# Row normalisation on one DMA queue: the order of loads and stores changed from alternating to runs of two

## The chip, the core and the metric

The kernel runs on one core of one Trainium2 chip. The metric is device time in microseconds (us) of one execution; lower is better. The core's engines that matter here are DVE (VectorE), ACT (ScalarE), SP (SyncE, which only issues transfers and waits) and the core's 16 DMA engines, which move the data between HBM and the on-chip memory SBUF.

## The reference: what is computed

```python
def reference(x):                      # x: 32 x 512 x 1024, float32
    sums = np.sum(np.abs(x), axis=-1, keepdims=True)
    return (x / (sums + 1e-8)).astype(np.float32)
```

Each of the 16384 rows of 1024 numbers is divided by the sum of its absolute values. x is 67.11 MB, and so is the output: every byte is read from HBM once and written once.

## The kernel before

**Tiling.** The 16384 rows are cut into 8 tiles (`ntiles`). One tile is 128 partitions x 16 rows (`R = 16`) x 1024 numbers: 8.39 MB, 64 KB in each partition, and contiguous in HBM. The tiles live in a pool of three buffers (`BUFS = 3`, line 29; pool, line 34), so tile 3 takes the buffer of tile 0, tile 4 that of tile 1, and so on: a tile's load may start only when the tile three before it has been stored. The result is written over the input in the same buffer.

**One tile's work.** `load(i)` (lines 70 to 78) issues the load on SP's queue (line 74) and then puts the tile's arithmetic, `normalize`, into the programs of DVE and ACT. DVE reduces all 16 rows to their sums of absolute values (line 40), adds 1e-8 (line 47), takes the reciprocal (line 49) and multiplies the first 8 rows by it (line 50). ACT multiplies the other 8 rows, one instruction a row (line 57), beside DVE's multiplication. `store(i)` (lines 80 to 84) issues the tile's store, also on SP's queue (line 82). The last tile, number 7, is cut into two halves of 8 rows by `span` (lines 64 to 66): two loads, two pieces of arithmetic, two stores. So there are 9 loads and 9 stores in all.

**What sets the order.** All transfers go through one queue, that of SP. SP takes its instructions in order: before a load it waits until the buffer's earlier store has landed, before a store until the tile's arithmetic is done, and whatever stands behind a waiting instruction waits too. Issued transfers go to the 16 DMA engines. The order is written out by hand as a list, `plan` (lines 88 to 95), and followed under `tc.manual_schedule()` (lines 97 to 102). With L for a load and S for a store, the list before is

```
L0 L1 L2  S0 S1  L3  S2  L4  S3  L5  S4  L6 L7  S5 S6 S7
```

Three loads come first; then a store and a load take turns; lines 94 and 95 swap the last load with the store ahead of it, so L7 stands directly behind L6. In this list a load is followed by a store at five places: L2 S0, L3 S2, L4 S3, L5 S4 and L7 S5. A store is followed by a load at four: S1 L3, S2 L4, S3 L5 and S4 L6. The arithmetic on DVE and ACT is in the order of the tiles, 0 to 7.

Of the kernel before, what the change touches and what calls it, by code (L numbers as in the profile page):

```python
# [1 line left out]

# [4 lines left out]

FP32 = mybir.dt.float32
EPS = 1e-8


@with_exitstack
def kernel(
    ctx: ExitStack,
    tc: tile.TileContext,
    x: bass.AP,
    out: bass.AP,
):
    nc = tc.nc
    P = nc.NUM_PARTITIONS  # L20

    x_flat = x.flatten_outer_dims()
    out_flat = out.flatten_outer_dims()
    n, d = x_flat.shape

    R = 16
    assert n % (P * R) == 0
    ntiles = n // (P * R)
    BUFS = 3

    x_t = x_flat.rearrange("(n p r) d -> n p r d", p=P, r=R)
    out_t = out_flat.rearrange("(n p r) d -> n p r d", p=P, r=R)

    sbuf = ctx.enter_context(tc.tile_pool(name="sbuf", bufs=BUFS))
    stats = ctx.enter_context(tc.tile_pool(name="stats", bufs=4))

    def normalize(x_tile, r0, k, kv):

        s = stats.tile([P, R], FP32)
        nc.vector.tensor_reduce(  # L40
            out=s[:, :k],
            in_=x_tile[:, r0 : r0 + k, :],
            axis=mybir.AxisListType.X,
            op=mybir.AluOpType.add,
            apply_absolute_value=True,
        )
        nc.vector.tensor_scalar_add(out=s[:, :k], in0=s[:, :k], scalar1=EPS)  # L47
        inv = stats.tile([P, R], FP32)
        nc.vector.reciprocal(out=inv[:, :k], in_=s[:, :k])  # L49
        nc.vector.tensor_mul(  # L50
            out=x_tile[:, r0 : r0 + kv, :],
            in0=x_tile[:, r0 : r0 + kv, :],
            in1=inv[:, :kv].unsqueeze(2).to_broadcast([P, kv, d]),
        )
        for r in range(kv, k):
            row = x_tile[:, r0 + r, :]
            nc.scalar.activation(  # L57
                out=row,
                in_=row,
                func=mybir.ActivationFunctionType.Copy,  # L60
                scale=inv[:, r : r + 1],
            )

    def span(i):
        k = R // 2 if i == ntiles - 1 else R
        return [(r0, k) for r0 in range(0, R, k)]

    tiles = {}

    def load(i):  # L70
        x_tile = sbuf.tile([P, R, d], FP32)
        tiles[i] = x_tile
        for r0, k in span(i):
            nc.sync.dma_start(
                out=x_tile[:, r0 : r0 + k, :], in_=x_t[i][:, r0 : r0 + k, :]
            )
        for r0, k in span(i):
            normalize(x_tile, r0, k, k // 2)

    def store(i):  # L80
        for r0, k in span(i):
            nc.sync.dma_start(  # L82
                out=out_t[i][:, r0 : r0 + k, :], in_=tiles[i][:, r0 : r0 + k, :]
            )

    plan = [("L", i) for i in range(BUFS)]
    for i in range(ntiles):
        plan.append(("S", i))  # L90
        nxt = i + BUFS - 1
        if BUFS <= nxt < ntiles:
            plan.append(("L", nxt))
    last = max(k for k, p in enumerate(plan) if p[0] == "L")
    plan[last - 1], plan[last] = plan[last], plan[last - 1]

    with tc.manual_schedule():
        for what, i in plan:
            if what == "L":
                load(i)  # L100
            else:
                store(i)


# [1 line left out]
_INS = ['x']  # L106
_OUTS = [((32, 512, 1024), 'float32')]


# [23 lines left out]
```

## Time and profile before

| | us |
|---|---|
| median of 4 runs (lowest to highest) | 318.94 (318.53 to 319.83) |
| the profiled execution's own time | 318.72 |
| its span, first to last instruction | 316.9 |
| time of the profiled execution outside the span | 1.8 |
| DVE busy (36 instructions) | 211.0, 67% of the span |
| ACT busy (65 instructions) | 68.8, 22% |
| DVE idle, waiting for a load to land (5 times) | 79.6 |
| one reduction of a whole tile, line 40 | 17.22 |
| one multiplication of 8 rows by DVE, line 50 | 8.69 |
| bytes moved (read plus written) | 134.2 MB |

The profile is one execution, taken by the hardware profiler. Its page gives each engine's busy time, a strip of 40 equal slices of the span with the busy share of the DMA engines and the GB/s they moved, the DMA queues, the chain of work that ended last, and the costliest groups of instructions. L40 is line 40 of the kernel. The trace behind the page can be asked for more: when each transfer was issued and how many us later it landed, what each engine waited for, and the busy times and GB/s in any stretch of the span that one chooses. "DMA share" in such a stretch is the mean busy share of the 16 engines; a packet is counted where it starts, so a share can come out a little above 1.

### The profile page before, as it was taken

Reading aid. Unit: us, or ns where it says so; the run is one execution under the profiler, and the core shown is the slowest. Engines: PE = TensorE matmul, PEld = TensorE weight load, DVE = VectorE, ACT = ScalarE, POOL = GpSimd, SP = SyncE. Lnnn points to the kernel's source line nnn. Section 1 sums busy time; section 2 is a strip of 40 time slices with the busy share of each in tenths; the row PEclk is TensorE's granted clock in tenths of the full one; section 3 lists DMA queues with packets and bytes.
Section 4 is the critical chain, followed back from the end, with each engine's and each line's share of the span. In section 5 each row is a group of like instructions: output and inputs, shape, how many; then the busy total and the mean of one; then the engine's idle time right before and its main releaser. Section 6 shows DMA issues by size and latency. Waiting matters only on the chain.

```text
span 316.9 us, 193 instructions
## 1 busy us (share of the span) xinstructions
DVE 211.0 (67%) x36; ACT 68.8 (22%) x65; POOL 0.2 (0%) x4
## 2 busy tenths in 40 slices
DVE  0019999999998007995089950899509999998000
ACT  0010081054028000055000550005400063415000
POOL 0000000000000000000000000000000000000000
DMA  9999999999999999999999999999999999999895
GB/s 397 397 397 488 438 397 405 389 447 480 397 397 505 422 397 414 505 405 397 414 455 455 397 455 414 447 405 455 430 397 443 426 473 414 447 422 447 380 451 244
DMA packets 2593, 134.23 MB, mean 424 GB/s; under 512 B 288, under 2 KB 288, under 8 KB 288
## 3 DMA queue, kind: packets, MB, share of 16 engines
q1 hardware_dynamic: 2592, 134.22, 98.7%
q14 instruction: 1, 0.01, 0.0%
HBM read 67.11 MB, written 67.11 MB: 423 GB/s over the span
## 4 chain that ended last, share of the span: by engine, by line
DVE 50%; DMA 29%; another core or an unknown queue 12%; issue 0%; DVEq 0%; SPq 0%
DVE s L40 33%; DMA x_tile<-in_x_dram 19%; DVE x_tile L50 17%; DMA out_dram<-x_tile 10%; DVE inv L49 1%; DVE s L47 0%; DVEq L50 0%; SPq L82 0%
## 5 line engine op out<-in xcount | busy, mean ns | idle before, releaser
L40 DVE TENSOR_REDUCE s<-x_tile 128x16 f32<-128x16384 f32 (+1 forms) x9 | 137.9, 15320 | 79.6 <-DMA x_tile<-in_x_dram 79.6
L57 ACT ACTIVATE x_tile<-x_tile,inv 128x1024 f32<-128x1024 f32 x64 | 67.5, 1136 | 200.1 <-DVE inv L49 190.7
L50 DVE TENSOR_TENSOR x_tile<-x_tile,inv 128x8192 f32<-128x8192 f32 (+1 forms) x9 | 69.7, 7744 | 0.6
L57 ACT ACT_TABLE_LOAD x1 | 1.3, 1283 | 22.7 <-DMA x_tile<-in_x_dram 22.7
L49 DVE RECIPROCAL inv<-s 128x16 f32<-128x16 f32 (+1 forms) x9 | 2.2, 242 | 0.3
L47 DVE TENSOR_SCALAR s<-s 128x16 f32<-128x16 f32 (+1 forms) x9 | 1.6, 174 | 0.3
L117 POOL MEMSET const-bfloat16-1.0<- 128x1 bf16 x1 | 0.1, 101 | 0.0
L117 POOL MEMSET const-uint8-127<- 128x1 uint8 x1 | 0.1, 101 | 0.0
L117 POOL MEMSET const-float32-0.0<- 128x1 f32 x1 | 0.1, 98 | 0.2 <-issue 0.2
L117 POOL MEMSET const-float32-1.0<- 128x1 f32 x1 | 0.1, 98 | 0.0
## 6 DMA issues: line engine op xcount, KB each, us to landing
x_tile<-in_x_dram SPq DMA_DIRECT2D x2, 4096.0 KB, 33.8
out_dram<-x_tile SPq DMA_DIRECT2D x2, 4096.0 KB, 26.1
x_tile<-in_x_dram SPq DMA_DIRECT2D x7, 51.3
out_dram<-x_tile SPq DMA_DIRECT2D x7, 32.3
```

Of the source, the lines that this page charges most:

```text
L40: nc.vector.tensor_reduce(out=s[:, :k], in_=x_tile[:, r0 : r0 + k, :], axis=mybir.AxisListType.X, op=mybir.AluOpType.add, apply_absolute_v ...
L47: nc.vector.tensor_scalar_add(out=s[:, :k], in0=s[:, :k], scalar1=EPS)
L49: nc.vector.reciprocal(out=inv[:, :k], in_=s[:, :k])
L50: nc.vector.tensor_mul(out=x_tile[:, r0 : r0 + kv, :], in0=x_tile[:, r0 : r0 + kv, :], in1=inv[:, :kv].unsqueeze(2).to_broadcast([P, kv, d]),)
L57: nc.scalar.activation(out=row, in_=row, func=mybir.ActivationFunctionType.Copy, scale=inv[:, r : r + 1],)
L117: nc = _bacc.Bacc("TRN2", target_bir_lowering=False, num_devices=1)
```

## The change

Only the list is built differently. After the three first loads, two stores and then two loads are appended, until nothing is left; the swap at the end is gone.

```diff
     plan = [("L", i) for i in range(BUFS)]
-    for i in range(ntiles):
-        plan.append(("S", i))
-        nxt = i + BUFS - 1
-        if BUFS <= nxt < ntiles:
-            plan.append(("L", nxt))
-    last = max(k for k, p in enumerate(plan) if p[0] == "L")
-    plan[last - 1], plan[last] = plan[last], plan[last - 1]
+    stored, loaded = 0, BUFS
+    while stored < ntiles:
+        for i in range(stored, min(stored + 2, ntiles)):
+            plan.append(("S", i))
+        stored = min(stored + 2, ntiles)
+        for i in range(loaded, min(loaded + 2, ntiles)):
+            plan.append(("L", i))
+        loaded = min(loaded + 2, ntiles)
```

The two lists, one under the other:

```
before  L0 L1 L2  S0 S1  L3  S2  L4  S3  L5  S4  L6 L7  S5 S6 S7
after   L0 L1 L2  S0 S1  L3 L4  S2 S3  L5 L6  S4 S5  L7  S6 S7
```

A load is now followed by a store at four places (L2 S0, L4 S2, L6 S4, L7 S6), and a store by a load at three (S1 L3, S3 L5, S5 L7). The transfers themselves, their sizes, the buffers and the arithmetic are the same. Between the landing of the last load and the end of the list there were three stores, S5, S6 and S7; now there are two.

## The prediction

> **What bounds the kernel now.** I read the page's strip of slices first, then the queue line, then the chain, then a table by stages.
>
> ```profile
> DVE  0019999999998007995089950899509999998000
> ...
> DMA  9999999999999999999999999999999999999895
> ...
> DMA packets 2593, 134.23 MB, mean 424 GB/s; under 512 B 288, under 2 KB 288, under 8 KB 288
> ...
> q1 hardware_dynamic: 2592, 134.22, 98.7%
> ```
>
> The reader is to see that the DMA row is nine tenths or more from the first slice nearly to the last, while DVE has holes. The queue's packets fill 98.7% of 16 engines' span: 0.987 x 316.9 = 312.8 us. The 4.1 us left lie before the first packet and after the last. So the DMA engines set the time, and DVE's 67% does not.
>
> The chain of waits gives landings (start plus duration): the first load 0.72 + 21.93 = 22.65, S0 49.20 + 32.56 = 81.76, L3 81.78 + 38.94 = 120.72.
>
> ```profile
> 0.72 21.93 DMA x_tile<-in_x_dram
> ...
> 49.20 32.56 DMA out_dram<-x_tile
> ...
> 81.78 38.94 DMA x_tile<-in_x_dram
> ```
>
> S0 waits 32.56 us and L3 38.94, though each is 8.39 MB: they stand in the queue behind others. The other landings I took from the view of x_tile's instructions over short windows, which gives one issue's time and its us to landing (L1: 1.1 + 40.9 = 42.0; L2: 1.6 + 60.8 = 62.4; S7's second half: 291.9 + 24.1 = 316.0). Cutting the span at these landings gives one stage for each transfer:
>
> ```profile
> 22.65:42.00 19.35, 19.22 (x4) 2.86 (x3) 0.00 (x0) 1.00 1.00 434
> 42.00:62.40 20.40, 20.40 (x2) 6.85 (x7) 0.00 (x0) 1.00 1.00 411
> 62.40:81.76 19.36, 19.26 (x5) 8.43 (x8) 0.00 (x0) 1.00 1.00 433
> 81.76:101.10 19.34, 19.24 (x4) 7.97 (x8) 0.00 (x0) 1.00 1.00 434
> 101.10:120.72 19.62, 0.72 (x1) 0.46 (x1) 0.00 (x0) 1.00 1.00 428
> 120.72:140.10 19.38, 19.19 (x4) 1.55 (x2) 0.00 (x0) 1.00 1.00 433
> 140.10:160.00 19.90, 7.15 (x1) 6.87 (x7) 0.00 (x0) 1.00 0.99 422
> 160.00:179.30 19.30, 19.11 (x4) 1.48 (x2) 0.00 (x0) 1.00 1.00 435
> 179.30:199.50 20.20, 7.22 (x1) 6.95 (x7) 0.00 (x0) 1.00 0.98 415
> 199.50:218.90 19.40, 19.20 (x4) 1.56 (x2) 0.00 (x0) 1.00 1.01 436
> 218.90:238.20 19.30, 7.14 (x1) 6.87 (x7) 0.00 (x0) 1.00 0.98 423
> 238.20:257.90 19.70, 19.49 (x4) 1.85 (x2) 0.00 (x0) 1.00 1.05 451
> ```
>
> The columns are the stretch, its length, busy DVE, ACT and POOL, clock, DMA share and GB/s. From the top: L1, L2, S0, S1, L3, S2, L4, S3, L5, S4, L6, L7. S5, S6 and S7 follow by 277.3, 296.7 and 316.0. The reader is to see two things. A transfer takes about 19.35 us (8.39 MB at 434 GB/s) whichever way it goes. And the longer ones are all loads with a store behind them: L2 is over by 1.05, L3 by 0.27, L4 by 0.55, L5 by 0.85, L7 by 0.35. A load behind a load (L1, L6), a store behind a load (S0), a store behind a store (S1) and a load behind a store (L6) cost no more than 19.36. So a turn from loading to storing has a price, 3.07 us over five, and the turn back has none I can see.
>
> **The change part by part.** *Bytes and instructions.* 9 loads and 9 stores, 36 DVE and 65 ACT instructions stay. A DMA issue on SP takes 0.33 to 0.43 us and their number is unchanged. Sum: 0.
>
> *Turns.* Five become four. L2 S0 stays as it is, 1.05: nothing ahead of it is moved. The three others (L4 S2, L6 S4, L7 S6) follow a pair of loads, or a lone load behind a pair of stores, and have no exact row. From below a turn costs 0.27, from above 1.05, by the rows. I take the mean of the four later turns, (0.27 + 0.55 + 0.85 + 0.35) / 4 = 0.505, since these stand in the same part of the run; L7's row, after the pair L6 L7, is the only one of that shape and is below it. New sum 1.05 + 3 x 0.505 = 2.57 against 3.07: **0.5 us less**. Bounds: 1.05 + 3 x 0.27 = 1.86, 1.2 less; 4 x 1.05 = 4.2, 1.1 more.
>
> *Does the queue ever run dry?* Laying the new list out with 19.35 a transfer and 0.5 a turn, from L2's landing at 62.4: S0 81.8, S1 101.1, L3 120.5, L4 140.3, S2 159.7, S3 179.0, L5 198.4, L6 218.2, S4 237.6, S5 256.9, L7 266.6 and 276.8 (halves), S6 296.1, S7 305.8 and 315.5. A transfer costs the end nothing if it is issued before the one ahead of it lands. A whole tile's arithmetic takes 17.22 + 0.2 + 0.3 + 8.69 = 26.5 us, a half 8.68 + 0.4 + 4.43 = 13.5; ACT's share lies beside DVE's multiplication.
> - L4 moves ahead of S2 on SP, and so S2 now stands behind L4's wait for S1 (101.1). S2's tile is ready at 101.8 (DVE's multiplication, 93.13 + 8.69), so the wait delays it by nothing. Both are in the queue by 102.7; L4 is needed at 120.5, S2 at 140.3.
> - S3: arithmetic 120.5 to 147.0, needed at 159.7. Cover 12.7.
> - L5 waits for S2 (159.7), needed at 179.0; L6 waits for S3 (179.0), needed at 198.4. Cover 19.
> - S4 stands behind L6's wait: ready at 173.5 (DVE takes it after tile 3), issued at 179.8, needed at 218.2. Held 6 us, and nothing waits for it.
> - S5: arithmetic 198.4 to 224.9, needed at 237.6. Cover 12.7. L7, two issues, waits for S4 (237.6), needed at 256.9.
> - S6 stands behind L7's wait and issues; arithmetic 224.9 to 251.4, needed at 276.8. Cover 25.
> - S7's halves: the first is loaded at 266.6 and done at 280.1, needed at 296.1; the second is done at 293.6, needed at 305.8. Cover 16 and 12.2. Here two stores hide the last tile's arithmetic where three did.
>
> Every cover is at least 12 us, so the waits cost 0. If one of these went, each us past the cover would be a us at the end. DVE's idle time for loads is rearranged: 22.7 + (120.5 - 101.8) + (198.4 - 173.5) + (266.6 - 251.4) = 81.5 in four waits, where 79.6 lay in five. It is off the path.
>
> *A rule.* Where a load is not followed by a store the rows show 19.30 to 19.40. The Trainium skill, "DMA: Bandwidth & Descriptors", section "Two DMAs through the same engine are not ordered", says that descriptors of one queue start in order but are pipelined, and that an engine's read and write sides are separate queues. Taken by itself that gives a turn no price, and this change then no gain: 318.94. The rows of L2 to L5 speak against it, and the measurement decides.
>
> *Sum.* Against the profiled execution: span 316.9 - 0.5 = 316.4, plus the 1.8 outside, 318.2. The median of the runs stands 0.22 above this execution (318.94 against 318.72), so 318.94 - 0.5 = **318.4**.
>
> **The rivals.** A difference of 0.3%, 0.96 us, is about what a measurement of this kernel can tell from no change; so beyond 317.98 or 319.90.
>
> *A turn is cheap when its store has stood in the queue for long.* For: S0, S3 and S4 were issued 13.2, 12.7 and 12.9 us before their turn (49.2 to 62.4, 147.3 to 160.0, 186.6 to 199.5) and those cost 1.05, 0.55 and 0.85; S2 and S5, issued 18.8 and 31.8 us before (101.9, 226.1), cost 0.27 and 0.35. In the new list the three stores stand 38, 38 and 25 us. Each would cost 0.31: 1.05 + 0.93 = 1.98, 1.1 less, 317.85, faster. Against: five points, and 0.55 to 1.05 at the same 13 us.
>
> *A turn is dear after a run of whole loads.* The dearest, L2 S0, is the only one after a run of whole-tile loads alone; 0.27 to 0.85 followed a single load. If runs of two put all engines to the turn in step as the run of three did, the three turns cost 1.05 each: 4.2, 1.1 more, 320.05, slower. It decides from 0.99 a turn. Against: L7 S5 came after L6 L7 and cost 0.35.
>
> *The queue runs dry.* It would happen first at S7's second half, where the cover is smallest. By the rows the arithmetic would have to end over 12.2 us late, and the longest of its instructions, 8.68, varies by nanoseconds. Priced at 1 us and more, slower; unlikely.
>
> *The change does not do what it says.* If the extra is not the turn's but each stretch's own (where in HBM it reads, say), five loads keep it: 0, and 318.94. That falls in the forecast's band.
>
> **How the numbers follow.** The forecast, with the last rival's zero in its band, 0.50, same (318.4; own range 318.0 to 319.3). The long-queued store 0.33, faster (317.85). The dear run 0.13, and the dry queue 0.04, both slower. So faster 0.33, same 0.50, slower 0.17. The range takes in both bounds of the turns, 318.94 - 1.2 and + 1.1, with a little below for the spread of the runs: 317.5 to 320.1.
>
> **What would show it.** Right: DMA row full, packets at about 98.7%, four long stages, the first 1.05 and the others near 0.5, all of them the load ahead of a store (L2, L4, L6, L7); DVE's idle time for loads near 81.5 in four waits. The first rival: those three near 0.3. The second: near 1. The dry queue: a slice of the DMA row under 9 before the end, or a store issued after the transfer ahead of it has landed. The whole argument is wrong if a stage that is not a load ahead of a store is long, for example the second of two loads or two stores.

## The result and the profile after

| | before | after |
|---|---|---|
| median, us (runs) | 319.64 (79) | 318.06 (53) |
| lowest to highest, us | 317.63 to 320.40 | 316.84 to 320.08 |
| the profiled execution, us (its span) | 318.72 (316.9) | 319.26 (317.5) |
| ratio after / before | | 0.9967, 95% interval 0.9958 to 0.9976 |

The ratio is 1.05 us of 319.64, between 0.77 and 1.34. It is a small gain, about one part in 300. The medians are 1.58 apart and the means 1.05 (319.32 and 318.27): the times of before lie in two heaps, around 318.3 and 319.8, and most are in the upper one, while most of those of after are below 318.7. The two profiled executions stand the other way round: that of before lies 0.9 below its median, that of after 1.2 above. So the two profiles cannot simply be subtracted; the spread of single executions, over 2.5 us in either column, is larger than the effect.

The page of the kernel after, its strip and queue line:

```profile
DVE  0019999999998007999998000999999702999100
...
DMA  9999999999999999999999999999999989999994
...
q1 hardware_dynamic: 2592, 134.22, 98.4%
```

The DMA row is as full as before; the single 8 is no empty queue, since the store in it had been issued long before. DVE now idles in fewer, longer stretches. The view of waits puts numbers on that (us in total, times, longest):

```profile
DVE s L40 <- DMA x_tile<-in_x_dram: 82.9, 4, 25.1
```

Four waits and 82.9 us, where 81.5 in four had been worked out. The table by stages of the kernel after, from L2's stage on, cut at its landings, which are read to about 0.1 us (stretch, length, DVE, ACT, POOL, clock, DMA share, GB/s):

```profile
42.00:62.30 20.30, 20.30 (x2) 6.88 (x7) 0.00 (x0) 1.00 1.01 413
62.30:81.78 19.48, 19.38 (x5) 8.42 (x8) 0.00 (x0) 1.00 0.99 431
81.78:101.55 19.77, 19.67 (x4) 8.39 (x8) 0.00 (x0) 1.00 0.98 424
101.55:120.88 19.33, 0.30 (x1) 0.04 (x1) 0.00 (x0) 1.00 1.00 434
120.88:140.80 19.92, 19.73 (x4) 2.09 (x2) 0.00 (x0) 1.00 0.98 421
...
160.26:179.70 19.44, 13.40 (x4) 8.42 (x8) 0.00 (x0) 1.00 1.00 432
179.70:198.92 19.22, 0.00 (x0) 0.00 (x0) 0.00 (x0) 1.00 1.01 436
198.92:219.50 20.58, 20.39 (x4) 2.75 (x3) 0.00 (x0) 1.00 1.03 443
...
258.20:277.90 19.70, 9.85 (x4) 0.80 (x1) 0.00 (x0) 1.00 1.05 452
```

The rows shown are L2, S0, S1, L3, L4, then S3, L5, L6, and last L7. Against 19.35: L5, which was over by 0.85 when a store stood behind it, is now followed by a load and takes 19.22. L6, which took 19.30 with a load behind it, is now followed by a store and takes 20.58. The extra goes where the turn goes. That answers the objection that the extra could belong to the stretch of HBM that a load reads. L3 is no such witness. It takes 19.33 here, and the 0.27 that the prediction gives it comes from a misread landing: S1 was issued at 75.5 and landed 25.9 us later, at 101.47 by the trace and not at 101.10. Cut there, S1 and L3 of the kernel before are

```profile
81.76:101.47 19.71, 19.61 (x4) 8.34 (x8) 0.00 (x0) 1.00 0.98 426
101.47:120.72 19.25, 0.35 (x1) 0.09 (x1) 0.00 (x0) 1.00 1.02 436
```

So S1, a store with a load behind it, is the long one of the two, over by 0.36 before and by 0.42 after, and L3 is not long in either.

### The profile page after: what moved, and what is told of

It is laid out like the page before. It is cut to its first block, busy times and chain, and to the rows that moved or that the text cites. A ratio compares the mean times of both kernels' runs of the same rounds, so it can differ in the third digit from the quotient of the medians.

```text
span 317.5 us, 193 instructions
## 1 busy us (share of the span) xinstructions
DVE 210.9 (66%) x36; ACT 68.8 (22%) x65; POOL 0.2 (0%) x4
## 4 chain that ended last, share of the span: by engine, by line
DMA 51%; DVE 33%; another core or an unknown queue 8%; SPq 0%; issue 0%; DVEq 0%
DMA x_tile<-in_x_dram 41%; DVE s L40 22%; DVE x_tile L50 11%; DMA out_dram<-x_tile 10%; DVE inv L49 0%; DVE s L47 0%; SPq L82 0%; DVEq L50 0%
## 5 line engine op out<-in xcount | busy, mean ns | idle before, releaser
L40 DVE TENSOR_REDUCE s<-x_tile 128x16 f32<-128x16384 f32 (+1 forms) x9 | 137.9, 15319 | 82.9 <-DMA x_tile<-in_x_dram 82.9
```

Of the source, the lines that this page charges most:

```text
L40: nc.vector.tensor_reduce(out=s[:, :k], in_=x_tile[:, r0 : r0 + k, :], axis=mybir.AxisListType.X, op=mybir.AluOpType.add, apply_absolute_v ...
```

## The experiments

All ratios are to the kernel before, run beside each version on the same chip, with their 95% intervals. "Extra" is what a profiled execution took from L1's landing to the last landing, less 14 transfers' worth of 19.35 us, 270.9. It is 3.1 us for before (316.0 - 42.0 - 270.9) and 3.7 for after (316.6 - 42.0 - 270.9). It is one draw each.

**One turn more.** The two lines that swap L7 ahead of S5 are taken out of the kernel before.

```diff
-    last = max(k for k, p in enumerate(plan) if p[0] == "L")
-    plan[last - 1], plan[last] = plan[last], plan[last - 1]
```

> The kernel before without the two lines that swap the last load with the store ahead of it: L0 L1 L2 S0 S1 L3 S2 L4 S3 L5 S4 L6 S5 L7 S6 S7, six turns from loading to storing in place of five. Theory of the turn's price (each such turn costs the end about 1 us, as one turn fewer gave 1.05): 1.0 us above before, ratio 1.003. Rival of the long queue (a turn is cheap, 0.3, where its store was issued long before, and 0.55 to 1.05 where it was issued about 13 us before): the new turn has S5 ready at 226 and needed at 238, and S6 now stands 13 us where S5 stood 32, so 0.8 for the new turn and 0.5 for the other: 1.3 us above, ratio 1.004. Rival of the place (the number of turns means nothing, only which transfers stand where at the end): between 0 and 0.3 us, ratio below 1.001.

Measured: 1.0022 (1.0004 to 1.0040), 318.82 against 318.13, so 0.7 us for the added turn; extra 3.5. One turn more is slower, as both the theory of the turn's price and the long queue say, at a lower price than either named, though the interval still holds 1.003 and ends at 1.004. It also holds the place theory's 1.001, so that one does not fall by this run alone.

**Two turns fewer.**

```diff
-            normalize(x_tile, r0, k, k // 2)
+            normalize(x_tile, r0, k, 4 if i < 2 else k // 2)
...
+    order = "L0 L1 L2 S0 S1 S2 L3 L4 L5 S3 S4 L6 L7 S5 S6 S7"
+    plan = [(w[0], int(w[1:])) for w in order.split()]
```

The first pair of lines moves rows of tiles 0 and 1 from DVE to ACT, so that S2's data are ready in time.

> Three turns: L0 L1 L2 S0 S1 S2 L3 L4 L5 S3 S4 L6 L7 S5 S6 S7, and for tiles 0 and 1 DVE multiplies 4 rows and ACT 12, so that tile 2 is done at about 93 when its store is needed at 101. By the rows of before no transfer is issued late (smallest cover 5 us, at S4). Theory of the turn's price: two turns fewer than before, 2.1 us less, ratio 0.9934, so 1.05 under the changed kernel. Rival of the long queue: L2 S0 1.05, L5 S3 0.85 (13 us in the queue), L7 S5 0.3, together 2.2 against 3.07: 0.9 less, ratio 0.997, no better than the changed kernel. Rival of the place: ratio 0.999 to 1.000.

Measured: 0.9961 (0.9945 to 0.9977), 316.95 against 318.13; extra 1.2. That is 1.24 us for two turns, 0.62 each. A price of 1.05 a turn (0.9934) is outside the interval, and so is the place theory (0.999 to 1.000); the long queue's 0.997 is inside. The stages L2, S2, L3, L4, L5, S4 and L7 of this kernel:

```profile
42.10:62.40 20.30, 20.23 (x4) 10.97 (x11) 0.00 (x0) 1.00 1.01 413
...
101.20:120.60 19.40, 0.00 (x0) 0.00 (x0) 0.00 (x0) 1.00 1.00 432
120.60:139.80 19.20, 0.00 (x0) 0.00 (x0) 0.00 (x0) 1.00 1.01 437
139.80:159.10 19.30, 19.10 (x4) 1.46 (x2) 0.00 (x0) 1.00 1.00 435
159.10:178.60 19.50, 19.50 (x2) 6.96 (x7) 0.00 (x0) 1.00 1.00 430
...
197.90:217.60 19.70, 19.54 (x4) 7.14 (x7) 0.00 (x0) 1.00 0.98 426
...
236.90:256.30 19.40, 19.24 (x4) 1.63 (x2) 0.00 (x0) 1.00 1.05 449
```

L2's turn stays at 0.95; L3 and L4, loads behind which a load follows, cost nothing; L5's turn is 0.15 and L7's 0.05. S4, a store with a load behind it, is over by 0.35. The long queue had 0.85 for L5 S3 (issued 12 us before its turn, 166.4 to 178.6): in this execution that row speaks against it.

**The stores issued late.** The changed kernel with work on ACT that holds back S2, S4 and S6 and nothing else.

```diff
+        for r in range({2: 23, 4: 26, 6: 12}.get(i, 0)):
+            row = x_tile[:, 8 + r % 8, :]
+            nc.scalar.activation(
+                out=row,
+                in_=row,
+                func=mybir.ActivationFunctionType.Copy,
+                scale=1.0,
+            )
```

> The changed kernel, with 23, 26 and 12 further ACT copies of a row onto itself behind tiles 2, 4 and 6, so that S2, S4 and S6 are issued 12 to 15 us before their turn where they stood 38, 38 and 25. Nothing else waits for them. Theory of the turn's price: as the changed kernel, 1.05 below before, ratio 0.9967. Rival of the long queue: the three turns cost 0.55 to 1.05 each, mean 0.82, together 1.05 + 2.45 = 3.5 against 3.07 in before: 0.4 above before, ratio 1.001.

Measured: 0.9991 (0.9973 to 1.0010), extra 3.2. The stores were issued 17, 20 and 15 us ahead of their turns, where 12 to 15 was meant. The interval just misses 0.9967 and just holds 1.001, and it overlaps the changed kernel's own. This run is undecided between the two, and leans to the long queue.

**No arithmetic, in both orders.** Whole tiles, only loaded and stored. Without the arithmetic a store no longer waits for anything but its load and its place on SP. The order shown is that of before; the other copy has the list of after.

```diff
-        for r0, k in span(i):
-            normalize(x_tile, r0, k, k // 2)
...
+    order = "L0 L1 L2 S0 S1 L3 S2 L4 S3 L5 S4 L6 L7 S5 S6 S7"
```

> The arithmetic is left out: whole tiles of 16 rows in three buffers, only loaded and stored, in the order of the kernel before without the cut of the last tile: five turns. Each store is issued when its load has landed, some 39 us before its turn. Theory of the turn's price: as before, 319.6, ratio 1.000. Rival of the long queue: five turns at 0.3 in place of 3.07 in all, 1.6 less, ratio 0.995.

> The same copy without arithmetic in the order of the changed kernel: four turns. Theory of the turn's price: about 1.0 us below the copy in the order of before. Rival of the long queue: 0.3 below it. If the gain came from the arithmetic's place beside the transfers: no difference between the two.

Measured: 0.9990 (0.9968 to 1.0012) in the order of before, extra 3.1; 0.9982 (0.9963 to 1.0000) in that of after, extra 2.4. The first excludes the 0.995 of the long queue. In the trace of the copy in the order of before, the stages L2, L4 and L5 (stretch, length, POOL, clock, DMA share, GB/s; DVE and ACT have no work here):

```profile
42.20:62.50 20.30, 0.00 (x0) 1.00 1.01 413
...
140.50:160.30 19.80, 0.00 (x0) 1.00 0.99 424
179.60:199.70 20.10, 0.00 (x0) 1.00 0.99 424
```

S0, S3 and S4 had stood about 39 us in the queue (22.7 to 62.5, 121.1 to 160.3, 160.3 to 199.7), and these turns cost 0.95, 0.45 and 0.75, much as in the kernel before (1.05, 0.55 and 0.85). So a turn does not need the arithmetic, and a long stand in the queue does not make it cheap. Between the two orders the medians differ by 0.2 us, within the intervals; the gain itself is not shown by this pair.

**Many turns, in small transfers.** The same copy in tiles of 4 rows and 12 buffers; G is 1 in the first and 8 in the second.

```diff
+    R = 4
...
+    BUFS = 12
...
+    G = 1
+    plan = [("L", i) for i in range(8)]
+    for i in range(0, ntiles, G):
+        plan += [("S", j) for j in range(i, i + G)]
+        plan += [("L", j) for j in range(i + 8, min(i + 8 + G, ntiles))]
```

> The arithmetic is left out: x is only loaded and stored. Tiles of 4 rows (2.10 MB, 32 tiles, 12 buffers), 8 loads first, then one store and one load in turn: 25 turns from loading to storing. Theory of the turn's price at 1 us a turn: 21 us above the copy with four turns; at the mean of the later rows of before, 0.5: 10.5 us. Rival of the long queue (all stores here are issued long before): 0.3 a turn, 6.3 us. If a turn has no price: no difference.

> The same copy without arithmetic in tiles of 4 rows, with stores and loads in runs of eight: 4 turns. The base for the copy with 25 turns. Every theory: bytes at 434 GB/s, 309.5 us, plus some 5 us of start and end inside the span and 1.8 outside, and 4 turns at 0.3 to 1 us: 318 to 321 us.

Measured: 321.10 with 25 turns (1.0069, 1.0048 to 1.0090) against 319.89 with four (1.0035, 1.0014 to 1.0056). That is 1.2 us for 21 turns, 0.06 each, far below every price that was named. The trace of the copy with 25 turns shows why the mean is so low; its rows in pairs, L7 and S0, L8 and S1, then L11 and S4, L12 and S5:

```profile
37.60:43.00 5.40, 0.00 (x0) 1.00 0.99 397
43.00:47.90 4.90, 0.00 (x0) 1.00 1.01 431
47.90:53.00 5.10, 0.00 (x0) 1.00 1.03 434
53.00:58.10 5.10, 0.00 (x0) 1.00 0.98 421
...
78.30:84.20 5.90, 0.00 (x0) 1.00 1.01 419
84.20:89.10 4.90, 0.00 (x0) 1.00 1.00 428
89.10:93.80 4.70, 0.00 (x0) 1.00 1.01 432
```

A transfer of this size takes some 4.85. The loads up to L11 are over by 0.2 to 1.0. From L12 (89.1 to 93.8) on the alternation costs nothing I can see: to the last landing a transfer takes 4.87 in the mean, where the copy with four turns takes 4.89. So the price is not a constant of each change of direction: it is paid over the first turns and then fades.

**Smaller packets at the turn.** The copies in small tiles had packets of 16 KB where the kernel has 64 KB, so the packet's size came next: every load ahead of a store is issued in two pieces, the second of two rows (8 KB packets), in the three orders, beside the changed kernel itself. The lines are those for the order of before; the order of after has tiles 2, 4, 6 and 7, that with three turns 2, 5 and 7.

```diff
+        pieces = span(i)
+        if i in (2, 3, 4, 5, 7):
+            r0, k = pieces.pop()
+            pieces += [(r0, k - 2), (R - 2, 2)]
+        for r0, k in pieces:
```

> The changed kernel itself, to stand on the same chip beside the three that follow. Every theory: ratio 0.9967 to 0.998, as it gave and as 0.6 to 0.7 us a turn (one turn more: 1.0022, two fewer: 0.9961) would have it.

> The kernel before, in its own order with five turns, but each load that stands ahead of a store (tiles 2, 3, 4, 5 and the second half of 7) is issued in two pieces, all rows but two and then two rows, so that the last packets ahead of the turn are of 8 KB and not of 64 or 32 KB. Theory of the packet (the price of a turn is a stretch of the one packet that each engine is moving there, and grows with its length: 1.06 for L2 with 64 KB packets, 0.33 in the copies with 16 KB packets, 0.02 to 0.1 for their other turns): of about 3 us of turns 2 go, less 0.1 us a cut for the added packets: 1.5 us less, ratio 0.995. Theory of the turn by itself (a price for each change of direction, whatever the packet): 0.3 us more for the added packets, ratio 1.001.

> The changed kernel with the same cut of the loads ahead of a store (tiles 2, 4, 6 and the second half of 7). Theory of the packet: about 0.3 us below the kernel before with the cut at most, since its one turn fewer is then worth little: ratio 0.994 to 0.995. Theory of the turn by itself: as the changed kernel, 0.2 us more, ratio 0.998.

> The order with three turns, and the cut of the loads ahead of a store (tiles 2, 5 and the second half of 7). Theory of the packet: L2's stretch falls from 1.06 to 0.3 or less and the other two were 0.1: 0.7 us below the order with three turns, ratio 0.994. Theory of the turn by itself: as the order with three turns, 0.9961 to 0.997. This would be the fastest of all kernels here by the theory of the packet.

Measured: the changed kernel again 0.9972 (0.9953 to 0.9992), extra 2.7; before with the cut 0.9994 (0.9975 to 1.0013), extra 3.3; after with the cut 0.9979 (0.9957 to 1.0001); three turns with the cut 0.9951 (0.9933 to 0.9968). For before the theory of the packet had 0.995, which the interval excludes, and L2's two pieces together, in the kernel before with the cut, take

```profile
42.00:62.70 20.70, 20.70 (x2) 6.86 (x7) 0.00 (x0) 1.00 1.01 412
```

1.35 over, no less than without the cut. The size of the load's packet does not set the price: that theory fell.

**The other side of the turn.** Three turns, with S0, S3 and S5 cut.

```diff
+        pieces = span(i)
+        if i in (0, 3, 5):
+            r0, k = pieces.pop(0)
+            pieces = [(0, 2), (2, k - 2)] + pieces
+        for r0, k in pieces:
```

> The order with three turns, with the cut on the other side of the turn: the stores that follow a load (S0, S3 and S5) are issued in two pieces, two rows and then fourteen, so that the first packets behind the turn are of 8 KB in place of 64 KB. The loads are whole. Theory of the store's packet (the copies with 16 KB packets on both sides lost 0.3 at their first turn, cutting the load alone left the 1 us of L2, so it is the packet behind the turn that sets the price): L2's stage falls from 20.4 us to 19.8 or less, and the time to 0.7 us below the order with three turns, ratio 0.994. Theory of the turn by itself (neither side's packet matters): L2's stage stays at 20.3 to 20.5 us, ratio 0.996 to 0.997.

Measured: 0.9974 (0.9955 to 0.9994), extra 1.6; L2's stage is 20.5 (42.1 to 62.6). The store's packet does not set it either. No cut is shown to help. The order with three turns, without a cut, has the lowest ratio of the plain orders. Against the changed kernel its lead (0.9961 beside 0.9967, not measured side by side) is not shown; with the cut it stood at 317.39 beside 317.88 on one chip, with overlapping intervals.

## Why the prediction was right or wrong

*What bounds the kernel:* right. The queue is full in both, and with 67% or 66% of DVE busy or with no arithmetic at all (0.9990 and 0.9982) the time is the same within 0.2%. The 4.1 us outside the queue's share are not all ahead of the first packet and behind the last: in the profile of before the 16 engines end one after another, from 313.2 to 315.7.

*The queue does not run dry:* right. The landings worked out (L4 140.3, L5 198.4, L6 218.2, S7 315.5) stand beside 140.8, 198.9, 219.5 and 316.6 in the profile after, and DVE's idle time fits to 1.4 us. Neither S2 behind L4's wait nor the loss of one cover at the end cost anything. The dry queue as a rival fell.

*A turn from loading to storing has a price:* right. L5 and L6 changed their lengths with what follows them, and the time goes with the number of turns: three 0.9961, four 0.9967 and 0.9972, five 1, six 1.0022. From six to three is 0.61%, 0.65 us a turn. Each order has one turn back fewer than turns, so the count alone cannot tell the two apart. The packets can. Each of the 16 engines moves a whole tile in eight packets of 64 KB. In all stretches below but one, just 16 packets start, the last one of each engine in one transfer, so the share times the length is the mean time of a packet. They are the ends of L2, S1 and L3 before; of L3 and L6 after, then a single packet of L6 on one engine; and of L5 with three turns:

```profile
57.80:58.60 0.80, 0.80 (x1) 0.00 (x0) 0.00 (x0) 1.00 4.37 1311
97.55:98.35 0.80, 0.80 (x1) 0.80 (x2) 0.00 (x0) 1.00 3.02 1311
116.85:117.75 0.90, 0.00 (x0) 0.00 (x0) 0.00 (x0) 1.00 2.88 1165
...
117.00:118.40 1.40, 0.00 (x0) 0.00 (x0) 0.00 (x0) 1.00 1.73 749
213.85:215.50 1.65, 1.65 (x1) 0.00 (x0) 0.00 (x0) 1.00 1.63 636
215.40:215.50 0.10, 0.10 (x1) 0.00 (x0) 0.00 (x0) 1.00 2.34 655
...
174.85:175.75 0.90, 0.90 (x1) 0.00 (x0) 0.00 (x0) 1.00 2.83 1165
```

A packet takes 2.42 us where no turn follows: so at S1, and at L3 after. Ahead of a store a load's last packets are longer: 3.50 at L2, 2.59 at L3 before, 2.69 at L6, 2.55 at L5. The single packet took 3.74 (2.34 x 0.10 x 16). So the turn from loading to storing is paid in the load's last packets. The turn back costs next to nothing: behind S1 a few packets were longer, 0.06 us an engine or less in both profiles. S1's extra is a late landing: it came 0.74 us (before) and 0.87 us (after) behind the store's last packet, where S0's came 0.36 and 0.37 behind, and L3's stage is the shorter for it. And a stage is as long as its slowest engine: L6's 1.23 is 0.27 in the mean and 1.3 on one engine, the one that ended that execution at 316.2, 1.8 us after the last of the other 15.

*The turns' sum, 0.5 us less:* too small; 1.05 was measured, and the two bounds, 1.2 less and 1.1 more, held it. That 318.4 stands beside a median of 318.06 is partly luck, since the median of before it was taken from, 318.94, was 319.64 over all runs. The term that was mis-sized is the 0.505 for each later turn. Two reasons are seen, and their shares are not separated. First, one execution gave the rows, and one execution is a draw: L6's turn cost 1.23 in one profile of the changed kernel and 0.55 (19.90, 198.2 to 218.1) in the other. The execution I read lay 0.9 below the later median of its kernel, so its turns were probably cheap ones; this is argued, not shown. Second, the rows were misread: with S1's landing at 101.47 L3 cost nothing, so its 0.27, and the bound 1.86 that rests on it, have no row behind them. S1 was then a long stage that is not a load ahead of a store, which the prediction had named as the sign that its whole argument is wrong; such stages stand in other runs too (S4 with three turns, over by 0.35, and S1 in the copy in the order of before, over by 0.45). Only the packets clear the turn back of it. By the packets (the time above 2.42, or above 1.21 for the half tiles' packets of 32 KB, in the mean of the engines) the turns of the two executions add up to 2.2 us before and 1.8 after. That is 0.4 of the 1.05; in what the rest lies, these two traces do not show.

*The forecast band, within 0.3%, at 0.50:* the measured 0.33% lies just past it, with an interval from 0.24% to 0.42% on both sides of the bound. The chance of 0.33 for faster was the one that came.

*The long-queued store:* its time, 317.85, is near the result, which is luck, since its mechanism is not what gives it. In the changed kernel S4 had stood 39 us (180.1 to 219.5) behind the longest of the later stages; the copy excludes its 0.995, and one of its two cheap points was the misread 0.27. Only the run with late stores leans its way, and that one is undecided.

*The dear run of whole loads:* fell as a time (slower by 1.1). L6, after a pair, did reach 1.23 in one execution, on one engine, but L4 (0.57, and in the second profile 0.0) and L7 (0.35) did not.

*The rule, by which a turn is free:* this was the prediction's reading of the Trainium skill, "DMA: Bandwidth & Descriptors", section "Two DMAs through the same engine are not ordered". For the first turns of every kernel here the rows speak against it; in the copy with 25 turns it holds from the sixth turn on.

What stays open is why those packets are longer. It needs neither the arithmetic, nor a short stand in the queue, nor large packets on one side of the turn. In the mean of the engines it is largest at the first turn (L2's stage is over by 0.95 to 1.35 in every kernel with 8.39 MB transfers) and smaller later, down to nothing in the alternating copy. That the 16 engines reach the first turn in step and drift apart later does not explain it alone: with three turns the last packets of L2 start within 0.65 us of each other and take 1.06 more than 2.42, those of L5 start within 0.77 us and take 0.13 more.

## What to carry to other kernels

When the transfer engines are full from end to end, cut the span at the landings of the transfers: equal lengths are the floor, and the few longer ones are all that an order of the same transfers can win. Before trusting such differences of tenths of a microsecond, read them in more than one execution, and in the packets as well as in the landings: a landing is that of the slowest engine and can itself come late. A median that lies off the profiled execution is a warning that its rows are cheap or dear ones. Fewer turns between loading and storing were worth about 0.2% each here, as long as every store's data were ready before its place in the queue came up.

## What the hardware showed that I had not expected

The price of a turn fades. In the copy with 25 turns the loads ahead of a store are over by 0.2 to 1.0 us up to L11, and the 20 turns after that cost nothing visible. It is paid in the last packets of a load, and in the profile of after one engine alone lost 1.3 us there and ended the kernel 1.8 us behind the rest. And small transfers are not free even in a full queue: the copy with four turns took 319.89 in pieces of 2.10 MB with 16 KB packets and 318.15 in pieces of 8.39 MB with 64 KB packets, on one chip, and its stages move about 430 GB/s where those of whole tiles move 434.
